# First pair of gate and up loads of each FFN block in eight half products, token sums made in stages

## The chip, the cores and the metric

The kernel runs on one core of one Trainium2 chip. The metric is the device time of one execution in microseconds; several timed runs are made, and their median counts. The engines are named as in the profile: PE (TensorE), DVE (VectorE), ACT (ScalarE), POOL (GpSimd), SP (SyncE, which issues the DMAs).

## The reference

The reference is one inference step of a decoder with two layers, on two groups of tokens: 512 prompt tokens and 64 tokens of samples with their states. A layer has four parts, each with a norm ahead and a residual add behind:

```python
x = x + 0.5 * swiglu(rmsnorm(x, ffn1_norm[l]), ffn1_w_gu[l], ffn1_w_down[l])
y, ... = even_mixer(...) or odd_mixer(...)      # on rmsnorm(x, mix_norm)
x = x + y
x = x + cross_attend(rmsnorm(x, xattn_norm[l]), mem_k[l], mem_v[l], xattn_wq[l], xattn_wo[l])
x = x + 0.5 * swiglu(rmsnorm(x, ffn2_norm[l]), ffn2_w_gu[l], ffn2_w_down[l])

def rmsnorm(x, g):
    return x * lax.rsqrt(jnp.mean(x * x, axis=-1, keepdims=True) + NORM_EPS) * g
def swiglu(x, w_gu, w_down):
    gate, up = jnp.split(x @ w_gu, 2, axis=-1)
    return (jax.nn.silu(gate) * up) @ w_down
```

The change touches the four calls of swiglu with the norm ahead of each. The model width is 1024 (8 chunks of 128), the hidden width 22 blocks of 128. All numbers are float32.

## The kernel before, in words

**Layout.** x stands transposed on the chip: xT has 8 chunks of 128 channels, each with 576 tokens, handled as two halves of TH = 288. A float32 product is made as three products of rounded parts: a number is split in a high part (ACT casts it to fp32r) and a low part (DVE subtracts the high part), and wh·xh + wh·xl + wl·xh is summed. One matmul is 128x128 by 128x288.

**FFN blocks.** There are four: A is ffn(0,1) at the start of the program, B is ffn(0,2) behind the output projection of layer 0's cross-attention, C is ffn(1,1) straight behind B's last down products, D is ffn(1,2) behind the cross-attention of layer 1. Each takes the 22 hidden blocks in parts (0,2), (2,6), ... (18,22). Two hidden blocks need a gate load and an up load, 1024x256 weights (1 MB) each, from two rotating buffers. `down` products (L1664) of a finished part are placed between the gate and up products of the next, and their results are added to xT by `add_x` (DVE, L1528).

**Seven products.** A load is multiplied with xT in a scheme of seven half-size products instead of eight (`seven`): the weights are seen as 2x2 blocks (odd and even chunks by the two column blocks), the tokens as blocks B11, B12, B21, B22 (odd and even chunk by token half). Seven weight forms (three blocks and four sums, the sums on DVE at L1609 and L1611) meet seven token forms: B11, T1, B21, T4, T2, B22 and T3, where the T are sums of blocks. Each product is `product` (L348): 12 matmuls, 4 chunk pairs by three parts; `seven` is 84 matmuls. DVE then puts the seven results together (L519 to L535, L1627, L1629). Each weight form is cast by ACT (L1578) and its low part made by DVE (L1579); forms rotate through two tags with three buffers each, so up to six are made ahead.

**Norm.** The tokens are not normalised ahead of the product: the products take x times the norm's gain, and the result is multiplied by rstd, the inverse root mean square. `norm_chunk` is called for a chunk as soon as xT's chunk is final: it makes the token forms (`token_forms`, all seven, 11 operations of DVE and 8 of ACT for a pair of chunks), and the square of x on ACT (L435), which POOL adds up into acc (L437; in A some on DVE). `norm_finish` multiplies acc by ones on PE (L479, which is behind the first two products of the FFN), takes Ln and Exp on ACT (L481, L482, each with a load of its function table), and corrects on DVE (L483, L485, L486). The gate result is multiplied by rstd (L519, L522), silu is taken on ACT (L526), and POOL multiplies by rstd once more (L528), for the up result that comes next (L532 to L535).

**Order.** `Stream` writes down a list of entries (one product or down product each) with posts (what DVE, ACT and POOL do with the results) and hooks; `emit` goes through it and `pin` ties the order on every engine. Behind each entry `make` makes forms ahead as far as buffers allow, and issues loads.

Of the kernel before, what the change touches and what calls it, by code (L numbers as in the profile page):

```python
# [140 lines left out]
class Net:  # L141
# [209 lines left out]
    def token_forms(self, c, name, base, late):  # L351
        nc = self.nc
        if c == 0:
            self.xf, self.late = {}, []
            for f in self.TOKENS_EARLY + self.TOKENS_LATE:
                h, l = (self.kp.tile([P, 2 * T], F32R, tag="y", bufs=6, name=self.nm("y")) if f in self.TOKENS_LATE else
                        self.kp.tile([P, 2 * T], F32R, tag=f"x{i}", bufs=4, name=self.nm("x")) for i in range(2))
                self.xf[f] = tuple(t.rearrange("p (j t) -> p j t", j=4) for t in (h, l))
        if c % 2 == 0:
            return  # L360
        j = c // 2
        (x11, x12), (x21, x22) = ((self.xT[:, k, :TH], self.xT[:, k, TH:]) for k in (c - 1, c))
        g1, g2 = self.vec(name, base + c - 1), self.vec(name, base + c)
        ta, tb = self.v2(self.ct('g1')), self.v2(self.ct('t0'))
        t1, t2, t4, t3 = ta[:, 0], ta[:, 1], tb[:, 0], tb[:, 1]

        def put(f, src, g):
            h, l = (t[:, j] for t in self.xf[f])
            if g is None:
                nc.scalar.copy(h, src)  # L370
                nc.vector.tensor_sub(l, src, h.bitcast(F32))
            else:
                nc.scalar.activation(h, src, AF.Identity, scale=g)
                nc.vector.scalar_tensor_tensor(l, src, g, h.bitcast(F32), ALU.mult, ALU.subtract)

        nc.vector.tensor_sub(t1, x12, x11)
        put('B11', x11, g1)
        nc.scalar.activation(t1, t1, AF.Identity, scale=g1)
        put('T1', t1, None)
        put('B21', x21, g2)  # L380
        nc.vector.scalar_tensor_tensor(t2, x22, g2, t1, ALU.mult, ALU.subtract)
        nc.vector.scalar_tensor_tensor(t4, x21, g2, t2, ALU.mult, ALU.subtract)
        put('T4', t4, None)

        def rest():
# [1400 lines left out]
```

## Time and profile before

| | us |
|---|---|
| timed runs | 3028.22, 3013.51, 3014.17 |
| their median | 3014.17 |
| the profiled execution's own time | 2999.72 |
| its span | 2997.9 |
| PE busy in it | 2866.5 (96%) |
| DVE busy | 2193.1 (73%) |
| ACT busy | 1280.0 (43%) |
| POOL busy | 419.8 (14%) |

The profile is of one execution, and its own time lies below the timed runs' median. The share of busy time is a mean over stages with different limits: the starts of the FFN blocks are at about 14, 995, 1400 and 2580 us of the span. The first gate load, first up load, second gate load and second up load of a block are called its first, second, third and fourth load. A start-to-end time of a run of instructions in the timeline (x24) includes what lies between them.

### The profile page before, as it was taken

To read this page: it belongs to the slowest core of one execution; us is meant where nothing else is said; L and a number is where in the kernel's file an instruction comes from. 1 tells how busy PE (TensorE), PEld (TensorE's weight loads), DVE (VectorE), ACT (ScalarE), POOL (GpSimd) and SP (SyncE) were. 2 spreads that over 40 slices of the span, in tenths; PEclk is the share of its full clock that TensorE was granted. 3 is DMA by queue.
4 is the path that set the end of the run, shared out by engine and by line. 5 is a ranking of instruction groups with operands and counts; after the bars stand their busy time and mean duration, and the time that the engine had idled before them with its cause. 6 is when DMAs were issued, how large, how long until landed. Compare 5 with 4: busy or idle time off the path is not lost.

```text
span 2997.9 us, 54618 instructions
## 1 busy us (share of the span) xinstructions
PE 2866.5 (96%) x22180; PEld 2707.4 (90%) x22180; DVE 2193.1 (73%) x3927; ACT 1280.0 (43%) x2302; POOL 419.8 (14%) x387
## 2 busy tenths in 40 slices
PE   5999999999999999997999999999999999999998
PEld 5999999999988899997999999988767787899998
DVE  7988866656556998887988875566577546898884
ACT  5544443222535544445444444433253534544443
POOL 1111011111100110001100011123222110110001
PEclk7999999999999999999999999999889999999999
DMA  3322232222445222221232232222113235232221
GB/s 113 111 93 85 89 85 72 72 82 93 145 167 175 75 95 92 87 87 61 89 99 89 89 96 78 81 60 81 38 34 92 86 142 192 73 97 89 92 81 64
DMA packets 343251, 278.76 MB, mean 93 GB/s; under 512 B 27332, under 2 KB 326168, under 8 KB 343000
## 3 DMA queue, kind: packets, MB, share of 16 engines
q1 hardware_dynamic: 343000, 275.27, 29.1%
q8 instruction: 175, 2.87, 0.4%
q14 instruction: 76, 0.62, 0.1%
HBM read 262.09 MB, written 13.14 MB: 92 GB/s over the span
## 4 chain that ended last, share of the span: by engine, by line
PE 81%; DVE 10%; ACT 4%; issue 2%; POOL 2%; DMA 1%; SPq 0%; ACTq 0%; POOLq 0%; DVEq 0%
PE pm L348 24%; PE pd L331 20%; PE pd L1664 17%; PE pd L348 4%; DVE wf L1579 2%; PE pm L968 1%; PE pm L891 1%; PE pd L1390 1%; PE pd L1359 1%; PE pd L1358 1%; PE pd L1360 1%; PE pm L1483 1%; PE pm L1452 1%; POOL acc L437 1%; PE pm L479 1%
## 5 line engine op out<-in xcount | busy, mean ns | idle before, releaser
L348 PE MATMUL pm<-x,wf 128*128 128x288 f32 x4224 | 606.8, 299 | 36.2 <-DVE wf L1579 14.5
L348 PEld LDWEIGHTS pm<-x,wf 128*128 128x128 f32 x4224 | 583.6, 191 | 41.9 <-DVE wf L1579 15.1
L331 PE MATMUL pd<-x,wh 128*128 128x288 f32 x2368 | 432.6, 302 | 0.0
L331 PEld LDWEIGHTS pd<-x,wh 128*128 128x128 f32 x2368 | 356.2, 191 | 5.4 <-ACT wh L317 0.9
L1664 PE MATMUL pd<-m,wf 128*128 128x288 f32 x2112 | 338.9, 296 | 12.1 <-DVE t L1629 8.2
L1528 DVE SCALAR_TENSOR_TENSOR xT<-pd,xT 128x576 f32<-128x576 f32 x240 | 181.2, 756 | 216.5 <-PE pd L1664 186.1
L1664 PE MATMUL pd<-g,wf 128*128 128x288 f32 x2112 | 337.5, 295 | 0.0
L528 POOL TENSOR_TENSOR g<-g,rstd 128x576 f32<-128x576 f32 x88 | 148.6, 1708 | 1271.9 <-DVE wf L1579 565.3
L1664 PEld LDWEIGHTS pd<-m,wf 128*128 128x128 f32 x2112 | 300.8, 188 | 14.2 <-ACT m L403 9.0
L348 PE MATMUL pm<-y,wf 128*128 128x288 f32 x2112 | 305.6, 295 | 0.3 <-ACT t L1625 0.3
L1664 PEld LDWEIGHTS pd<-g,wf 128*128 128x128 f32 x2112 | 299.2, 188 | 0.2
L348 PEld LDWEIGHTS pm<-y,wf 128*128 128x128 f32 x2112 | 289.5, 188 | 0.9 <-ACT t L1625 0.8
L1578 ACT CAST wf<-raw 128x512 fp32r<-128x512 f32 x264 | 163.1, 620 | 290.3 <-PE pd L1664 161.2
L331 PE MATMUL pd<-x,wl 128*128 128x288 f32 x1184 | 261.7, 302 | 0.0
L1578 ACT CAST wf<-t 128x512 fp32r<-128x512 f32 x264 | 163.8, 622 | 207.4 <-PE pm L348 82.4
L317 ACT CAST wh<-raw 128x1024 fp32r<-128x1024 f32 x106 | 111.1, 1048 | 274.2 <-PE pd L331 248.4
L1579 DVE TENSOR_TENSOR wf<-raw,wf 128x512 fp32r<-128x512 f32 x264 | 204.7, 776 | 11.3 <-ACT wf L1578 11.3
L1579 DVE TENSOR_TENSOR wf<-t,wf 128x512 fp32r<-128x512 f32 x264 | 193.2, 732 | 7.4 <-ACT wf L1578 7.4
L331 PEld LDWEIGHTS pd<-x,wl 128*128 128x128 f32 x1184 | 193.6, 191 | 1.8
L1578 ACT CAST wf<-S 128x512 fp32r<-128x512 f32 (+1 forms) x192 | 112.6, 587 | 161.4 <-PE pm L348 77.2
L331 PE MATMUL pd<-y,wh 128*128 128x288 f32 x896 | 169.6, 305 | 0.3 <-DVE xT L1528 0.3
L348 PE MATMUL pd<-y,wf 128*128 128x288 f32 x1056 | 155.8, 295 | 2.8 <-DVE wf L1579 2.8
(529 smaller groups left out, 4863.0 us busy)
## 6 DMA issues: line engine op xcount, KB each, us to landing
raw<-ffn_w_gu SPq DMA_DIRECT2D x88, 1024.0 KB
S<-ffn_w_down SPq DMA_DIRECT2D x160, 256.0 KB
raw<-xattn_wkv SPq DMA_DIRECT2D x16, 1024.0 KB
x<-cache_mem_v SPq DMA_DIRECT2D x32, 512.0 KB
raw<-cache_mem_k SPq DMA_DIRECT2D x16, 1024.0 KB
raw<-odd_w_in SPq DMA_DIRECT2D x30, 512.0 KB
raw<-even_w_in SPq DMA_DIRECT2D x16, 512.0 KB
raw<-xattn_wq SPq DMA_DIRECT2D x8, 1024.0 KB
```

The costliest lines, as they stand in the source:

```text
L317: nc.scalar.copy(h, raw[:, :, c:c + step])
L331: nc.tensor.matmul(ps[:, hf, :TH], w[:, k], x[:, hf * TH:(hf + 1) * TH], start=(k == 0 and w is wh and xi == 0), stop=(k == nk - 1 and w i ...
L348: self.nc.tensor.matmul(ps, a[:, j], b[:, j], start=(not more and j + i == 0), stop=(j == n - 1 and i == 2), skip_group_check=more)
L437: eng.tensor_add(self.acc, self.acc, sq)
L479: nc.tensor.matmul(ps[hf][:, :TH], lhsT, sq[:, hs])
L528: nc.gpsimd.tensor_mul(t, t, self.rstd)
L891: self.nc.tensor.matmul(ps[:, :TH], lhsT, rhs[:, hf * TH:(hf + 1) * TH])
L968: self.nc.tensor.matmul(ps[q, c * 64:(c + 1) * 64], *fn(c, q))
L1528: self.nc.vector.scalar_tensor_tensor(x, ps, s, x, ALU.mult, ALU.add)
L1578: self.nc.scalar.copy(h, src)
L1579: self.nc.vector.tensor_sub(l, src, h.bitcast(F32))
L1664: nc.tensor.matmul(ps[:, hf, :TH], a[:, k], b[:, hf * TH:(hf + 1) * TH], start=(k + i == 0), stop=(k == nk - 1 and i == 2))
```

## The change

In each FFN block the first pair of loads is multiplied in the plain way (`plain`, new): for each of the two column blocks, two half products (odd and even chunks), each with both token halves, so eight half products of 12 matmuls for a load (four entries of 24). It needs the four plain token blocks and four weight forms, no sums of weights. The gate's two halves gather in a double bank (psd) and are scaled by one operation of 576 elements, the up's in two single banks.

`norm_chunk` makes only the plain blocks (`token_blocks`: 4 operations of DVE and 4 of ACT for two chunks). The token sums T1, T2, T4 and T3 are made in eight stages (`token_sums`) as posts of the first pair's entries, the last two in the second gate load. silu is taken for each column block apart, and the first hidden blocks are split in the third load. The norm's matmuls go to two psm banks, and stand behind the second entry (A: the third). In A all sums of squares are on DVE. Hooks run ahead of posts.

```diff
-    TOKENS_EARLY, TOKENS_LATE = ('B11', 'T1', 'B21', 'T4'), ('T2', 'B22', 'T3')
-    def token_forms(self, c, name, base, late):
...
+    def token_blocks(self, c, name, base):
         if c == 0:
+            self.xf = {f: self.token_tiles(f, True) for f in ('B11', 'B12', 'B21', 'B22')}
+            self.xg = name, base
+        g, x = self.vec(name, base + c), self.xT[:, c]
+        for f, src in ((f'B{1 + c % 2}1', x[:, :TH]), (f'B{1 + c % 2}2', x[:, TH:])):
+            self.form_hi(self.xf, f, c // 2, src, g)
+            self.form_lo(self.xf, f, c // 2, src, g)
+    def token_sums(self, xf):
...
+        def first():
+            xf.update({f: self.token_tiles(f, False) for f in ('T1', 'T2', 'T4')})
+            d['t'] = [self.v2(self.ct('g1')) for _ in four]
+            for j in four:
+                nc.vector.tensor_sub(d['t'][j][:, 0], x[2 * j][1], x[2 * j][0])
+                nc.scalar.activation(d['t'][j][:, 0], d['t'][j][:, 0], AF.Identity, scale=g[2 * j])
+
+        def second():
+            for j in four:
+                t = d['t'][j]
+                self.form_hi(xf, 'T1', j, t[:, 0])
+                nc.vector.scalar_tensor_tensor(t[:, 1], x[2 * j + 1][1], g[2 * j + 1], t[:, 0], ALU.mult, ALU.subtract)
...
+        def seventh():
+            xf['T3'] = self.token_tiles('T3', True)
+            for j in four:
+                t = d['t'][j][:, 1]
+                nc.vector.scalar_tensor_tensor(t, x[2 * j][0], g[2 * j], t, ALU.mult, ALU.subtract)
+                self.form_hi(xf, 'T3', j, t)
...
-            ps = [self.psm(), self.psm()]
+        ps = [self.psm(1 if paired else None), self.psm(1 if paired else None)]
...
+                if t is None:
+                    nc.vector.tensor_mul(self.v2(z[n]), a, self.v2(self.rstd))
...
             if m0 == 0:
-                hooks = {1: finish, 6: loads} if then else {1: finish}
+                ts = [lambda n=n: steps[n]() for n in range(8)]
+                st.plain(wg, x, gate, [[ts[0]], [ts[1]], [], [ts[2], lambda: gated(0)]], {2: finish, 3: loads} if then else {1: finish}, False)
+                st.plain(wu, x, up, [[], [lambda: gated(1), ts[3]], [ts[4]], [ts[5]]], {}, True)
+                st.waiting += [(9, ts[6]), (10, done), (11, ts[7])]
+                return
...
-            self.square(c, self.nc.gpsimd if c % 3 == 1 else self.nc.vector)
+            self.square(c, self.nc.vector)
...
+    def plain(self, src, x, put, posts, hooks, single):
...
+                    for j in range(4):
+                        for i in range(3):
+                            for t in range(2):
+                                xs = x[row + str(t + 1)]
+                                self.nc.tensor.matmul(d['ps'][t][:, :TH], (wh, wh, wl)[i][:, j], xs[i == 1][:, j],
+                                                      start=(k + j + i == 0), stop=(k == 1 and j == 3 and i == 2))
...
             self.pin(e['run'], e['form']['w'])
-            post(e['posts'])
             if e['hook']:
                 e['hook']()
+            post(e['posts'])
             self.make(k)
```

Lines move by the change: L1528 becomes L1566, L1578 and L1579 become L1616 and L1617, L1611 becomes L1649, L479 becomes L509, L483 to L486 become L513 to L516, L532 (the up result times the gate's) becomes L566. New are L367 (low part of a plain block), L365 (low part of a sum), L389 and L396 (first two token sums), L549 (the gate's scaling of a whole block), and L1710 (the matmul of `plain`).

**Where the instructions move.** First, DVE at the end of B, where the last down products of B are added to xT and C's norm is fed. Between two residual adds (xT<-pd) stood, before, the token forms of a pair of chunks (x and y are their tiles, g and t scratch):

```order
L1528 SCALAR_TENSOR_TENSOR xT<-pd_14989,xT 128x576
L374 SCALAR_TENSOR_TENSOR x_14917<-xT,vecn,x_14916 128x288
L381 SCALAR_TENSOR_TENSOR g_15044<-xT,vecn,g_15044 128x288
L374 SCALAR_TENSOR_TENSOR x_14921<-xT,vecn,x_14920 128x288
L371 TENSOR_TENSOR x_14919<-g_15044,x_14918 128x288
L382 SCALAR_TENSOR_TENSOR t_15045<-xT,vecn,g_15044 128x288
L371 TENSOR_TENSOR y_14925<-g_15044,y_14924 128x288
L374 SCALAR_TENSOR_TENSOR y_14927<-xT,vecn,y_14926 128x288
L388 SCALAR_TENSOR_TENSOR t_15045<-xT,vecn,g_15044 128x288
L371 TENSOR_TENSOR x_14923<-t_15045,x_14922 128x288
L1528 SCALAR_TENSOR_TENSOR xT<-pd_15018,xT 128x576
```

Now, in the same place (xf are tiles of token blocks, wf weight forms, raw the gate load of C's first pair):

```order
L1566 SCALAR_TENSOR_TENSOR xT<-pd_14908,xT 128x576
L1617 TENSOR_TENSOR wf_15088<-raw_15081,wf_15088 128x512
L367 SCALAR_TENSOR_TENSOR xf_14859<-xT,vecn,xf_14858 128x288
L367 SCALAR_TENSOR_TENSOR xf_14861<-xT,vecn,xf_14860 128x288
L1566 SCALAR_TENSOR_TENSOR xT<-pd_14941,xT 128x576
L1617 TENSOR_TENSOR wf_15091<-raw_15081,wf_15091 128x512
L367 SCALAR_TENSOR_TENSOR xf_14855<-xT,vecn,xf_14854 128x288
L367 SCALAR_TENSOR_TENSOR xf_14857<-xT,vecn,xf_14856 128x288
L1566 SCALAR_TENSOR_TENSOR xT<-pd_14974,xT 128x576
```

Nine operations on 288 tokens stood between two adds; now there are three, and one of them is a weight form of the next block.

Second, DVE in B around the first operation on rstd. Before (acc's result is pd_10617):

```order
L371 TENSOR_TENSOR y_10061<-g_10507,y_10060 128x288
L374 SCALAR_TENSOR_TENSOR y_10063<-xT,veca,y_10062 128x288
L388 SCALAR_TENSOR_TENSOR t_10508<-xT,veca,g_10507 128x288
L371 TENSOR_TENSOR x_10059<-t_10508,x_10058 128x288
L1611 TENSOR_TENSOR t_10581<-g_10576,raw_10554 128x512
L371 TENSOR_TENSOR y_10065<-t_10508,y_10064 128x288
L1579 TENSOR_TENSOR wf_10583<-t_10560,wf_10583 128x512
L483 SCALAR_TENSOR_TENSOR t_10616<-rstd_10615 128x576
L485 SCALAR_TENSOR_TENSOR t_10616<-pd_10617,t_10616 128x288 x2
L486 SCALAR_TENSOR_TENSOR rstd_10615<-t_10616,rstd_10615 128x576
L1611 TENSOR_TENSOR t_10627<-raw_10554,t_10581 128x512
```

Now:

```order
L389 TENSOR_TENSOR g_10523<-xT 128x288
L513 SCALAR_TENSOR_TENSOR t_10557<-rstd_10556 128x576
L515 SCALAR_TENSOR_TENSOR t_10557<-pm_10558,t_10557 128x288
L515 SCALAR_TENSOR_TENSOR t_10557<-pm_10559,t_10557 128x288
L516 SCALAR_TENSOR_TENSOR rstd_10556<-t_10557,rstd_10556 128x576
L396 SCALAR_TENSOR_TENSOR g_10520<-xT,veca,g_10520 128x288
L396 SCALAR_TENSOR_TENSOR g_10521<-xT,veca,g_10521 128x288
L396 SCALAR_TENSOR_TENSOR g_10522<-xT,veca,g_10522 128x288
L396 SCALAR_TENSOR_TENSOR g_10523<-xT,veca,g_10523 128x288
L1649 TENSOR_TENSOR t_10579<-g_10484,raw_10479 128x512
L1617 TENSOR_TENSOR wf_10581<-raw_10465,wf_10581 128x512
L549 TENSOR_TENSOR g_10609<-pd_10489,rstd_10556 128x576
```

The token forms stood ahead of rstd; now a subtraction of token halves stands there, and the scaled sums (L396) and the gate's scaling (L549) follow behind it.

Third, PE in B around the norm's matmuls on acc. Before, they stood behind two products of 12 with token tiles x and banks pm:

```order
L348 MATMUL pm_10599<-x_10054,wf_10567 128x288 x2
L348 MATMUL pm_10599<-x_10055,wf_10567 128x288
L348 MATMUL pm_10599<-x_10054,wf_10567 128x288
L479 MATMUL pd_10617<-acc_10051,cblob 128x288 x2
L348 MATMUL pm_10586<-x_10056,wf_10570 128x288
L348 MATMUL pm_10586<-x_10057,wf_10570 128x288
```

Now, behind two entries of 24 in the double bank pd_10489 and ahead of the second column block's, pd_10584:

```order
L1710 MATMUL pd_10489<-xf_10028,wf_10470 128x288
L1710 MATMUL pd_10489<-xf_10025,wf_10470 128x288
L1710 MATMUL pd_10489<-xf_10027,wf_10470 128x288
L509 MATMUL pm_10558<-acc_10020,cblob 128x288
L509 MATMUL pm_10559<-acc_10020,cblob 128x288
L1710 MATMUL pd_10584<-xf_10021,wf_10473 128x288
L1710 MATMUL pd_10584<-xf_10023,wf_10473 128x288
L1710 MATMUL pd_10584<-xf_10022,wf_10473 128x288
```

There are 24 matmuls ahead of the norm's in B before, and 48 now.

## Rows read from the trace of the kernel before

**Rows 1.** The page's part 1: busy us (share) xinstructions, by engine.
```profile
PE 2866.5 (96%) x22180; PEld 2707.4 (90%) x22180; DVE 2193.1 (73%) x3927; ACT 1280.0 (43%) x2302; POOL 419.8 (14%) x387
```

**Rows 2.** Windows: stretch, its us, busy (xinstructions) by engine, PEclk, DMA, GB/s.
```profile
14.00:70.00 56.00, 31.32 (x175) 27.88 (x172) 47.08 (x90) 35.82 (x68) 8.71 (x5) 0.70 0.25 78
...
995.50:1029.07 33.57, 26.15 (x174) 24.37 (x173) 29.87 (x48) 21.12 (x38) 8.54 (x5) 0.95 0.13 43
...
1029.00:1098.00 69.00, 68.93 (x507) 68.96 (x508) 67.77 (x123) 32.18 (x62) 7.76 (x4) 0.98 0.31 100
```

**Rows 3.** Waits of PE: waiting <- released by: us, times, longest us.
```profile
PE pd L479 <- POOL acc L437: 16.6, 3, 8.9
...
PE pm L348 <- DVE wf L1579: 14.5, 2, 11.9
...
PE pd L1664 <- DVE xT L1528: 2.2, 2, 1.2
```

**Rows 4.** Timeline of PE in A: start, us, line, operation, [idle before <-releaser].
```profile
17.79 0.85 PE L348 MATMUL pm<-x,wf 128*128 128x288 f32 x2 [3.65 <-ACT wf L1578]
...
45.26 2.29 PE L479 MATMUL pd<-acc,cblob 128*128 128x288 f32 x4 [8.94 <-POOL acc L437]
...
70.19 5.08 PE L348 MATMUL pm<-x,wf 128*128 128x288 f32 x25 [1.87 <-DVE g L532]
```

**Rows 5.** Timeline of PE in B, a later down product last.
```profile
995.53 3.35 PE L348 MATMUL pm<-x,wf 128*128 128x288 f32 x24
...
1002.73 2.29 PE L479 MATMUL pd<-acc,cblob 128*128 128x288 f32 x4 [3.85 <-POOL acc L437]
...
1029.07 8.15 PE L348 MATMUL pm<-x,wf 128*128 128x288 f32 x48 [1.86 <-DVE g L532]
...
1099.29 0.96 PE L1664 MATMUL pd<-m,wf 128*128 128x288 f32 x6
```

**Rows 6.** Timeline of PE at the start of C.
```profile
1400.36 0.43 PE L348 MATMUL pm<-x,wf 128*128 128x288 f32 x2
...
1412.66 4.48 PE L348 MATMUL pm<-x,wf 128*128 128x288 f32 x22 [11.87 <-DVE wf L1579]
...
1416.97 1.13 PE L479 MATMUL pd<-acc,cblob 128*128 128x288 f32 x4
...
1442.35 6.62 PE L348 MATMUL pm<-x,wf 128*128 128x288 f32 x48 [1.40 <-DVE g L532]
```

**Rows 7.** Chain of waits in B: start, us, what.
```profile
1043.61 3.20 PE pm L348 x24
```

**Rows 8.** Timeline of ACT in B's norm.
```profile
1005.10 1.28 ACT L481 ACT_TABLE_LOAD   x1 [0.42 <-PE pd L479]
...
1008.60 0.69 ACT L482 ACTIVATE rstd<-t 128x576 f32<-128x576 f32 x1
```

**Rows 9.** Timeline of DVE in A, B and C.
```profile
50.50 0.76 DVE L483 SCALAR_TENSOR_TENSOR t<-rstd 128x576 f32<-128x576 f32 x1 [6.84 <-ACT rstd L482]
...
992.97 1.19 DVE L371 TENSOR_TENSOR y<-g,y 128x288 fp32r<-128x288 f32 x3
...
994.20 1.38 DVE L374 SCALAR_TENSOR_TENSOR y<-xT,veca,y 128x288 fp32r<-128x288 f32 x3
...
1009.39 0.76 DVE L483 SCALAR_TENSOR_TENSOR t<-rstd 128x576 f32<-128x576 f32 x1 [3.24 <-ACT rstd L482]
...
1022.99 1.92 DVE L1579 TENSOR_TENSOR wf<-t,wf 128x512 fp32r<-128x512 f32 x1
...
1042.05 0.76 DVE L1528 SCALAR_TENSOR_TENSOR xT<-pd,xT 128x576 f32<-128x576 f32 x1 [0.24 <-PE pd L1664]
...
1098.35 0.68 DVE L1579 TENSOR_TENSOR wf<-S,wf 128x512 fp32r<-128x512 f32 x1
...
1413.12 1.28 DVE L1579 TENSOR_TENSOR wf<-raw,wf 128x512 fp32r<-128x512 f32 x2
...
1422.48 0.76 DVE L483 SCALAR_TENSOR_TENSOR g<-rstd 128x576 f32<-128x576 f32 x1 [5.54 <-ACT rstd L482]
```

More of the change, by code (lines that the diff above doesn't have):

```diff
@@ L349, in product @@
                                       stop=(j == n - 1 and i == 2), skip_group_check=more)
-    def token_forms(self, c, name, base, late):
-        nc = self.nc
-        if c == 0:
[L354 to L385, printed above, removed]
-            put('T2', t2, None)
-            put('B22', x22, g2)
-            nc.vector.scalar_tensor_tensor(t3, x11, g1, t2, ALU.mult, ALU.subtract)
-            put('T3', t3, None)
-        self.late.append(rest)
-        if c == KD - 1 or not late:
-            for r in self.late:
-                r()
-            self.late = []
@@ new lines, in token_tiles, with form_hi @@
+    def token_tiles(self, f, plain):
+        h, l = (self.kp.tile([P, 2 * T], F32R, tag=f"x{i}" if plain else "y", bufs=4 if plain else 6,
+                             name=self.nm("xf")) for i in range(2))
+        return tuple(t.rearrange("p (j t) -> p j t", j=4) for t in (h, l))
+    def form_hi(self, xf, f, j, src, g=None):
+        h = xf[f][0][:, j]
+        if g is None:
+            self.nc.scalar.copy(h, src)
+        else:
+            self.nc.scalar.activation(h, src, AF.Identity, scale=g)
@@ L405, in split, with norm_chunk @@
         return h, l
-    def norm_chunk(self, c, name, base, squares=True, late=False):
+    def norm_chunk(self, c, name, base, squares=True):
         nc = self.nc
@@ L498, in ffn @@
         st = Stream(self)
-        x, rest = {}, []
+        x, rest, steps = {}, [], []
         def loads():
@@ L568, in ffn @@
         x.update(self.xf)
+        steps.extend(self.token_sums(x))
         st.emit()
@@ L1646, in seven, with make, run @@
                 self.place(job)
+    def plain(self, src, x, put, posts, hooks, single):
+        net = self.net
+        u = dict(src=src, steps=4, first=len(self.forms))
+        self.units.append(u)
+        for n in range(2):
+            d = {}
+            for k in range(2):
+                def make(tag, n=n, k=k):
+                    v = u['raw'].rearrange("p (j two) f -> p two j f", two=2)
+                    return self.form(v[:, k, :, n * P:(n + 1) * P], tag)
+                def run(w, n=n, k=k, d=d):
+                    if not k:
+                        if single:
+                            d['ps'] = [net.psm(n), net.psm(n)]
+                        else:
+                            d['pd'] = net.psd()
+                            d['ps'] = [d['pd'][:, 0], d['pd'][:, 1]]
+                    (wh, wl), row = w, f'B{k + 1}'
+                    for j in range(4):
[4 more added lines that the diff above has]
+                                                      start=(k + j + i == 0), stop=(k == 1 and j == 3 and i == 2))
+                e = self.entry(dict(make=make), run, hooks.get(2 * n + k))
+                self.entries[e]['posts'] += posts[2 * n + k]
+            if single:
+                for t in range(2):
+                    self.pending.append(lambda n=n, d=d, t=t: put(n, t, d['ps'][t][:, :TH], None, None))
+            else:
+                self.pending.append(lambda n=n, d=d: put(n, None, d['pd'][:, :, :TH], None, None))
     def full(self, src, xin, nk, m, add):
```

63 lines of the change are left out of this document (45 added, 18 removed).

## The prediction

> **What bounds the kernel now.** I read the page's busy line first, then the waits of TensorE (PE), then the four FFN starts in PE's timeline, then windows over them, and last VectorE's (DVE's) timeline. The four FFN blocks are called A (program start), B, C and D here.
>
> PE is busy 96% of a span of 2997.9 us [rows 1], so the kernel as a whole can only gain where PE stops. The list of its waits [rows 3] has two of the longest at FFN starts: PE waits 16.6 us in 3 waits for the sum of squares (acc, L437), and 14.5 us in 2 for weight forms (L1579). In time order they stand at A (8.94 us before L479), B (3.85), C (11.87 before the second part of its first product) [rows 4 to 6]; what is left of the 16.6, 3.8 us, is D, which is laid out like B.
>
> Why PE stops there is seen in the windows [rows 2]: between the end of the product ahead of B and B's third load, 33.57 us, PE works 26.15 us and DVE 29.87; in the 69 us that follow DVE works 67.77. So an FFN start is a stretch in which DVE makes token forms, weight sums and the low halves of weights, and PE is held by that list; after it DVE has no slack for some 70 us. At B its weight form of 1098.35 ends at 1099.03, and the down product that reads it starts at 1099.29: a lead of 0.26 us [rows 9, 5]. What counts is therefore not PE's own earliest time but how much earlier DVE reaches the point from which both kernels have the same DVE order, the weight forms of the fourth load.
>
> **What the change costs on PE.** Seven half products of 12 matmuls become eight in two loads of four FFNs: 2 × 12 × 4 = 96 matmuls more. 24 of them take 3.20 us back to back [rows 7], 0.133 us each: +12.8 us of PE work. It falls wholly into the stretches with the stops, 3.2 us in each.
>
> **What it does to DVE and ScalarE ahead of rstd.** Before, a pair of chunks costs 11 DVE operations ahead of the norm, now 4; the first pair's 8 weight sums in each FFN go, and of 14 forms 8 stay. The sums over tokens come after, in steps. The norm's two matmuls (L479, now L509) stand behind 48 half-product matmuls in B, C and D, behind 72 in A.
>
> B: the first product starts at 995.53 [rows 5] as before, since it needs only plain blocks. 48 × 0.133 = 6.4, so L509 comes at 1001.9; acc, held before by the longer list on DVE and ScalarE, is there by then. L509 takes 1.13 us at full clock (its row in C) [rows 6]. Then ScalarE: from the table load at 1005.10 to the end of Exp at 1009.29 are 4.2 us, of which the first 1.28 us table load waited for PE and now has time ahead of it; 2.9 stay [rows 8]. With 0.6 for the handovers, DVE's first operation on rstd starts at 1006.5 where it was 1009.39 [rows 9]: 2.9 us earlier. D the same.
>
> C: the nine DVE operations between two residual adds become three, so the two stops of PE for xT (2.2 us [rows 3]) go, nearly: 1.7. The first product then starts at 1398.7 in place of 1400.36 and does not stop for 11.87 us, as its four forms are made from the raw load in the tail. L509 at 1405.1, plus 1.1, 2.9 and nothing else late: rstd at 1409.1 where it was 1422.48 [rows 9]: 13.4 us earlier.
>
> A: the plain blocks of all chunks stand ahead of the first form, so I put the first product at 20.0 (17.79 before [rows 4]). 72 matmuls are 9.6 us at full clock. In the window 14 to 70 the mean granted clock was 0.70 [rows 2], and after the stop at 45.26 the four L479 matmuls took 2.29 us, against 1.13 in C: PE there ran at the lower level, 1.2 GHz, after idling. I add 2.8 us for such a beginning, 1 for late token blocks: L509 at 33.4, rstd on DVE at 33.4 + 1.1 + 2.9 = 37.4, I take 37.6 against 50.50 [rows 9]: 12.9 us earlier. If all 72 run at the lower level it is 6.8 us less.
>
> **What it costs behind rstd.** From rstd to the fourth load's second form DVE had 53 operations, now 60: nine 128x512 fewer, two 128x288 tensor operations, twelve 128x288 scalar-tensor-tensor and two 576-wide ones more. By rows with several in a run [rows 9] these are 0.64, 0.40, 0.46 and 0.76 us (the single 576-wide row): -5.8 + 0.8 + 5.5 + 1.5 = +2.1 us. Both ends: +0.8, if GpSimd's multiplications meet one operation fewer (the form at 1022.99 beside one took 1.92 us, 1.28 more than 0.64), and +4.7 if they meet two more. I take +1.5, nearer the lower end, because a run of two or three shows the overlap of neighbours only in part, and the removed kind is the longest. In A four of the scalar-tensor-tensor and two 128x512 stand ahead of rstd: 4 × 0.46 + 2 × 0.64 = 3.1 less behind it.
>
> On what these meetings cost, the Trainium skill ("SBUF — State Buffer", section "Who interferes with whom") says that a VectorE instruction with two SBUF inputs contends with a GpSimd one that reads SBUF, the port pair being an exclusive lock. The row of 1022.99 agrees in kind. The new scalar-tensor-tensor operations have two SBUF inputs too, so by that rule the change exposes more of DVE's list: if each of the eight first-pair multiplications cost one further 1.28 us, the sum would be 20 in place of 30 us and the median 2994.
>
> Moved work that I cost at nothing: the split of the first hidden blocks now stands in the third load, ahead of downs that start later; loads are issued no later, since a plain load frees its buffer after four forms; in A the constants' DMAs move three entries ahead, and SP waits there anyway for buffers. If that cover is gone PE waits at the third load, as it does today for L532 (1.86 us at 1029.07 [rows 5]); I keep that wait in all four.
>
> **The sum**, at the fourth load: A 12.9 + 3.1 - 1.5 = 14.5; C 13.4 - 1.5 = 11.9; B and D 2.9 - 1.5 = 1.4 each, plus the 0.24 us that DVE idled at 1042.05 and the lead of 0.26 [rows 9], 1.9 each. Together 30.2 us. That the gain is kept: PE and DVE move together from there, in the same order. PE alone does not limit it: B's 192 matmuls and L509 end at 995.53 + 25.5 + 1.1 = 1022.2, with the 1.9 wait 1024.1, 5.0 earlier than 1029.07; C at 1398.7 + 26.6 + 1.9 = 1427.2, 15.1 earlier than 1442.35; A at 20.0 + 2.8 + 1 + 26.6 + 1.9 = 52.3, 17.9 earlier than 70.19 [rows 4 to 6].
>
> The profiled execution took 2999.72 us, its span 2997.9; by its rows the new one takes about 2969.5. The timed runs have a median of 3014.17 (3013.51 to 3028.22), 14 above it, so the median forecast is 3014.17 - 30.2 = 2984.
>
> **Rivals.**
> 1. DVE gives more back: +4.7 behind rstd in place of +1.5. A 11.3, C 8.7, B and D below zero by 1.3 each: 17.4 us, 2997. For it: DVE's 67.77 of 69 us. Against: at B the list has only two GpSimd multiplications to meet, as before. Between this and the forecast lies 2990.
> 2. PE sets the end, because forms are made up to six ahead and DVE catches up where ScalarE or PE released it late: 17.9 + 5.0 + 15.1 + 5.0 = 43 us, 2971. For it: 0.24 us of idle time shows that PE paces DVE a little. Against: a lead of 0.26 us.
> 3. The slower side: the granted clock falls at FFN starts. Eight products with waits between them (two psm banks for the up product, each released by L566) leave PE short stops; where it then runs at 1.2 GHz, a matmul costs 0.133 us more. 227 matmuls at that level eat the 30.2 us; all 192 of each of B, C and D would cost 76.8, 3061. For it: the 24 matmuls and L479 after stops in A and B ran at the lower level, and 48 matmuls after the 1.86 us stop took 8.15 us where C took 6.62 after 1.40 [rows 5, 6]. Against: the stops removed are the long ones (8.94, 11.87, 3.85).
> 4. The stops do not go, only move behind the third load, since rstd is not what DVE waits for: then the 12.8 us are paid and nothing is won, 3027, within what counts as no change.
>
> **How the numbers follow.** Forecast 0.50, rival 1 0.20, rival 2 0.13, rival 3 0.06, rival 4 0.11. A measurement of this kernel can tell about 0.5%, 15 us, from no change: faster means below 2999, slower above 3029. The forecast and rival 2 are faster, and most of rival 1: 0.50 + 0.13 + 0.18 = 0.81. Same: rival 4 and the rest of 1, 0.13. Slower: rival 3, 0.06. The forecast's own range is 2976 to 2992 (A's clock, the two ends behind rstd); with rivals 1 and 2 it reaches 2968 to 3004, which leaves out rivals 3 and 4.
>
> **What would show it.** Right: no wait for acc or weight forms over 1 us at the starts of B, C and D; DVE's rstd operation near 37.6, 1006, some 13 us earlier in C's own frame, with a list of about 32.5 us behind it; PE work up by 12.8 us and its idle time down by about 43. Wrong: a wait for L566 or L365 above 3 us in the first pair, a clock below 0.9 in B's first 30 us, or a new wait for weight forms in the 70 us behind the third load, which would mean that the gain is given back there.

## The result, and the profile after

| | before | after |
|---|---|---|
| median of the timed runs, us | 3014.8 (3013.51 to 3028.22) | 2978.12 (2972.74 to 2981.82) |
| ratio after/before, 95% interval | | 0.9867 (0.9833 to 0.9901) |
| the profiled execution, its span | 2999.72, 2997.9 | 2981.82, 2980.0 |

The change is faster by 1.3%. The forecast was 2984 us, 30 us less than before; the medians differ by 36.7 us, the two profiled executions by 17.9. In the profiled pair the block starts gain 29.4 us and the two mixers give part of it back, as is shown below; of the other timed runs there is no trace.

The page's part 1 of the new profile (busy us, share of the span, instructions by engine), which answers to [rows 1]:

```profile
PE 2882.4 (97%) x22276; PEld 2725.2 (91%) x22276; DVE 2128.0 (71%) x3842; ACT 1266.0 (42%) x2278; POOL 419.9 (14%) x384
```

PE works 15.9 us more. 12.8 were worked out from 96 matmuls, but 10.4 of the 15.9 lie in the mixer of layer 1 (783.92 against 773.55 us in the rows of e0 below), which has the same 6697 matmuls in both and ran at a lower granted clock. The span is 17.9 us shorter, and PE's idle time fell from 131.4 to 97.6 us. DVE works 65 us less.

The windows of A's start and, from B's first product, 33.57 us, answering to the first two of [rows 2] (columns: stretch, its us, busy of PE, PEld, DVE, ACT, POOL, PEclk, DMA share, GB/s):

```profile
14.00:70.00 56.00, 45.93 (x301) 44.67 (x300) 49.61 (x95) 37.81 (x74) 4.50 (x3) 0.88 0.31 98
985.22:1018.79 33.57, 31.96 (x238) 31.53 (x237) 27.22 (x51) 20.81 (x39) 7.66 (x3) 1.00 0.16 52
```

In B's stretch PE works 31.96 us where it worked 26.15, and its granted clock is 1.00 where it was 0.95; in A's the clock is 0.88 where it was 0.70.

PE's waits (us in total, times, longest us), answering to [rows 3]:

```profile
PE pm L347 <- DVE g L566: 11.1, 5, 4.5
...
PE pm L347 <- ACT t L1663: 4.6, 3, 1.5
...
PE pd L347 <- DVE xf L365: 3.6, 4, 0.9
...
PE pm L347 <- ACT wf L1616: 3.2, 4, 0.8
...
PE pm L509 <- DVE acc L471: 1.1, 1, 1.1
```

The waits for acc at the FFN starts (16.6 us) and for weight forms (14.5) are gone, and that for xT in C's tail; 1.1 us for acc is left, in A. The program's first product still waits 3.3 us for ScalarE's cast. The wait for the up result has grown (L566, 11.1 us in 5, four of them at the starts, where L532 had 7.5 us in 5), and, not foreseen, there are three kinds of short ones in the third and fourth loads.

PE at the starts of A, B (its last row is the down product that answers to the last of [rows 5]) and C:

```profile
17.42 12.34 PE L1710 MATMUL pd<-xf,wf 128*128 128x288 f32 x72 [3.25 <-ACT wf L1616]
30.81 1.24 PE L509 MATMUL pm<-acc,cblob 128*128 128x288 f32 x4 [1.06 <-DVE acc L471]
...
52.51 11.91 PE L347 MATMUL pm<-xf,wf 128*128 128x288 f32 x72 [4.53 <-DVE g L566]
```

```profile
985.22 6.53 PE L1710 MATMUL pd<-xf,wf 128*128 128x288 f32 x48
991.60 1.14 PE L509 MATMUL pm<-acc,cblob 128*128 128x288 f32 x4
...
1013.45 8.25 PE L347 MATMUL pm<-xf,wf 128*128 128x288 f32 x60 [1.61 <-DVE g L566]
...
1086.46 0.96 PE L1737 MATMUL pd<-m,wf 128*128 128x288 f32 x6
```

```profile
1385.62 6.53 PE L1710 MATMUL pd<-xf,wf 128*128 128x288 f32 x48
1391.99 1.14 PE L509 MATMUL pm<-acc,cblob 128*128 128x288 f32 x4
...
1413.93 8.26 PE L347 MATMUL pm<-xf,wf 128*128 128x288 f32 x60 [1.70 <-DVE g L566]
```

In C the first product now runs without a stop into the norm, where it waited 11.87 us [rows 6]; in B the norm's matmuls wait for nothing, where they waited 3.85 [rows 5]. What is left in these rows are the stops ahead of the third load: 4.53 us in A, 1.61 in B, 1.70 in C.

DVE in A, B and C: the first operation on rstd in each, and rows of B ahead of it and behind it, answering to [rows 9]:

```profile
37.78 0.76 DVE L513 SCALAR_TENSOR_TENSOR t<-rstd 128x576 f32<-128x576 f32 x1 [3.51 <-ACT rstd L512]
```

```profile
988.16 1.93 DVE L1617 TENSOR_TENSOR wf<-raw,wf 128x512 fp32r<-128x512 f32 x1
...
996.61 0.76 DVE L513 SCALAR_TENSOR_TENSOR t<-rstd 128x576 f32<-128x576 f32 x1 [5.05 <-ACT rstd L512]
...
1008.26 2.96 DVE L407 SCALAR_TENSOR_TENSOR g<-xT,veca,g 128x288 f32<-128x288 f32 x4
1012.24 0.69 DVE L1617 TENSOR_TENSOR wf<-raw,wf 128x512 fp32r<-128x512 f32 x1 [1.02 <-ACT wf L1616]
...
1028.71 0.68 DVE L1617 TENSOR_TENSOR wf<-g,wf 128x512 fp32r<-128x512 f32 x1
...
1030.62 0.74 DVE L1566 SCALAR_TENSOR_TENSOR xT<-pd,xT 128x576 f32<-128x576 f32 x1
```

```profile
1397.10 0.76 DVE L513 SCALAR_TENSOR_TENSOR g<-rstd 128x576 f32<-128x576 f32 x1 [5.05 <-ACT rstd L512]
```

From B's first product to DVE's operation on rstd are now 996.61 - 985.22 = 11.39 us, before 1009.39 - 995.53 = 13.86. In C it is 11.48, before 22.12; in A 20.36, before 32.71.

**Where the time came from.** The same event stands in both traces, so the lead of the new kernel can be followed from place to place:

| event (PE or DVE) | before, us | after, us | lead, us |
|---|---|---|---|
| A's first residual add | 83.67 | 70.53 | 13.1 |
| B's first FFN product | 995.53 | 985.22 | 10.3 |
| a down product of B | 1099.29 | 1086.46 | 12.8 |
| C's first FFN product | 1400.36 | 1385.62 | 14.7 |
| ninth residual add of C | 1512.84 | 1488.76 | 24.1 |
| D's first FFN product | 2579.56 | 2563.50 | 16.1 |
| ninth residual add of D | 2685.14 | 2666.53 | 18.6 |

The four starts gain 13.1 (A), 2.5 (B), 24.08 - 12.83 = 11.2 (C, with B's tail), and 2.6 (D, 18.61 - 16.06): 29.4 us. Between them, in the mixers and cross-attention, 2.8 us of the lead went in layer 0 and 8.0 in layer 1. The change edits no line of the mixers.

### The profile page after: what moved, and what is told of

Its sections match the earlier page's. It is cut to its first block, busy times and chain, and to the rows that moved or that the text cites. A ratio compares the mean times of both kernels' runs of the same rounds, so it can differ in the third digit from the quotient of the medians.

```text
span 2980.0 us, 54645 instructions
## 1 busy us (share of the span) xinstructions
PE 2882.4 (97%) x22276; PEld 2725.2 (91%) x22276; DVE 2128.0 (71%) x3842; ACT 1266.0 (42%) x2278; POOL 419.9 (14%) x384
## 4 chain that ended last, share of the span: by engine, by line
PE 82%; DVE 9%; ACT 4%; issue 2%; POOL 1%; DMA 1%; SPq 0%; ACTq 0%; POOLq 0%; DVEq 0%
PE pm L347 23%; PE pd L331 21%; PE pd L1737 18%; PE pd L347 4%; DVE wf L1617 2%; PE pm L1006 2%; PE pm L929 1%; PE pd L1428 1%; PE pd L1397 1%; PE pd L1396 1%; PE pd L1398 1%; PE pm L1521 1%; PE pm L1490 1%; PE pm L1506 1%; DVE xf L365 1%
## 5 line engine op out<-in xcount | busy, mean ns | idle before, releaser
L347 PE MATMUL pm<-xf,wf 128*128 128x288 f32 x5760 | 807.3, 296 | 19.0 <-DVE g L566 11.1
L347 PEld LDWEIGHTS pm<-xf,wf 128*128 128x128 f32 x5760 | 781.5, 188 | 22.5 <-ACT wf L1616 16.1
L1566 DVE SCALAR_TENSOR_TENSOR xT<-pd,xT 128x576 f32<-128x576 f32 x240 | 181.2, 755 | 253.7 <-PE pd L1737 189.8
L1616 ACT CAST wf<-raw 128x512 fp32r<-128x512 f32 x272 | 166.9, 619 | 300.3 <-PE pd L1737 168.1
L1616 ACT CAST wf<-t 128x512 fp32r<-128x512 f32 x240 | 149.0, 622 | 200.3 <-PE pm L347 76.2
L1617 DVE TENSOR_TENSOR wf<-raw,wf 128x512 fp32r<-128x512 f32 x272 | 208.9, 770 | 15.2 <-ACT wf L1616 15.0
L1617 DVE TENSOR_TENSOR wf<-t,wf 128x512 fp32r<-128x512 f32 x240 | 174.3, 726 | 10.3 <-ACT wf L1616 10.3
L1616 ACT CAST wf<-S 128x512 fp32r<-128x512 f32 (+1 forms) x192 | 112.6, 587 | 157.9 <-PE pm L347 69.2
L347 PE MATMUL pd<-xf,wf 128*128 128x288 f32 x960 | 141.9, 295 | 3.6 <-DVE xf L365 3.6
L331 PEld LDWEIGHTS pd<-y,wh 128*128 128x128 f32 x896 | 136.7, 193 | 4.0 <-DVE xT L1566 0.5
L318 DVE TENSOR_TENSOR wl<-raw,wh 128x1024 fp32r<-128x1024 f32 x106 | 130.6, 1232 | 10.9 <-ACT wh L317 6.9
```

The lines of the kernel that those rows point to most:

```text
L318: nc.vector.tensor_sub(l, raw[:, :, c:c + step], h.bitcast(F32))
L331: nc.tensor.matmul(ps[:, hf, :TH], w[:, k], x[:, hf * TH:(hf + 1) * TH], start=(k == 0 and w is wh and xi == 0), stop=(k == nk - 1 and w i ...
L347: self.nc.tensor.matmul(ps, a[:, j], b[:, j], start=(not more and j + i == 0), stop=(j == n - 1 and i == 2), skip_group_check=more)
L1566: self.nc.vector.scalar_tensor_tensor(x, ps, s, x, ALU.mult, ALU.add)
L1616: self.nc.scalar.copy(h, src)
L1617: self.nc.vector.tensor_sub(l, src, h.bitcast(F32))
```

## The experiments

All runs are measured in the same way: a block's frame is the time from its first product (PE, L1710) to its first residual add (DVE, L1566), in B 1030.62 - 985.22 = 45.40 us; beside it stands the time to DVE's first operation on rstd (L513). Frames of the changed kernel repeat to a tenth of a microsecond between two profiles, while its timed executions differ by up to 19 us.

| kernel | frame A | B | C | D | rstd A | B | C | D |
|---|---|---|---|---|---|---|---|---|
| after | 53.11 | 45.39 | 45.48 | 45.39 | 20.36 | 11.39 | 11.48 | 11.39 |
| e0, the same again | 53.16 | 45.40 | 45.48 | 45.39 | 20.36 | 11.39 | 11.48 | 11.40 |
| e1, later norm | 53.15 | 45.29 | 45.30 | 45.26 | 20.37 | 13.34 | 13.34 | 13.34 |
| e2, 24 matmuls fewer | 53.13 | 44.34 | 45.45 | 45.38 | 20.37 | 10.32 | 11.48 | 11.40 |
| e3, earlier norm | 51.05 | 42.22 | 42.33 | 42.24 | 17.21 | 8.21 | 8.30 | 8.21 |
| e4, list shortened | 53.15 | 43.69 | 44.44 | 43.68 | 20.37 | 11.40 | 11.48 | 11.40 |
| e5, squares on GpSimd | 54.95 | 45.40 | 45.49 | 45.39 | 22.17 | 11.40 | 11.48 | 11.39 |
| e7, e3 and T4's stage later | 51.06 | 41.18 | 41.28 | 41.19 | 18.26 | 8.22 | 8.31 | 8.22 |
| e8, e7 and the square first | 50.65 | 40.34 | 40.33 | 40.35 | 17.85 | 7.37 | 7.37 | 7.38 |

**e0, b0, b1: what one and the same kernel does.** No edit: the changed kernel once more, the kernel before twice more.

> The changed kernel once more, unedited. Frame used for all runs: from a block's first half product to the start of the first residual add inside the block (A 53.1, B 45.4, C 45.5, D 45.4 us in the first profile). Theory 1 (the block starts are set by DVE's list behind rstd, and the 11 us given back between B's end and D's start in the first profile are the clock of that one execution): the four frames repeat within 0.3 us, while the stretches of the two mixers differ by several us between profiles of one and the same kernel. Theory 2 (the change itself delays the mixers, by the norm's new banks or the DMA order): the mixers come out as late against the kernel before as in the first profile, 2.8 us in the first and 8 us in the second.

> The kernel before once more, unedited. Frames are taken from a block's first FFN product to the first residual add inside the block, and were 65.9, 46.5, 54.6 and 46.5 us in A, B, C, D in the first profile; the sum of what the change gains at the four starts and in C's tail was 29.4 us, while the medians of the timed runs differ by 37 us. Theory 1: the frames repeat within 0.5 us, and the rest of the difference lies in the two mixers (outside the FFN blocks), at a lower granted clock there: this profile is longer than the first by that alone. Rival: the frames of the kernel before vary by several us, and the first profile was a fortunate one.

> The kernel before a third time, for the same question: frames within 0.5 us of 65.9, 46.5, 54.6, 46.5 by theory 1; the mixers' stretches (0.4 to 0.95 ms and 1.77 to 2.56 ms) differ by several us between the three profiles of one and the same kernel.

The frames repeat, for the changed kernel within 0.1 us; for the kernel before they are 65.5, 45.8, 55.5 and 45.8 in b0 (3013.8 us) and 65.5, 46.2, 54.8 and 46.2 in b1 (3006.1 us), against 65.9, 46.5, 54.6 and 46.5: within 0.9, not the 0.5 expected. This bears on the sum of the gains: with the same changed profile, taken from A's first residual add and from the ninth adds of B, C and D, the four starts gain 12.7, 0.6, 12.9 and 0.6 us against b0 (26.8 in all) and 12.7, 1.0, 11.4 and 1.0 against b1 (26.2). In B and D the first profile, from which the forecast was worked out, was the slowest of the three.

The mixer of layer 1 does not repeat. From a residual add at C's end to D's first product, in five profiles (before, b0, b1, after, e0):

```profile
1771.44:2579.56 808.12, 773.55 (x6697) 669.44 (x6696) 503.37 (x1003) 332.83 (x600) 156.61 (x179) 0.95 0.29 88
```

```profile
1774.09:2595.74 821.65, 788.11 (x6697) 680.84 (x6696) 503.23 (x1003) 333.09 (x600) 155.92 (x179) 0.93 0.29 87
```

```profile
1772.30:2588.55 816.25, 779.71 (x6697) 674.47 (x6696) 502.87 (x1003) 332.95 (x600) 155.34 (x179) 0.94 0.29 88
```

```profile
1747.36:2563.50 816.14, 783.92 (x6697) 679.14 (x6696) 489.41 (x979) 329.02 (x591) 158.96 (x181) 0.94 0.29 88
```

```profile
1746.48:2546.47 799.99, 766.88 (x6698) 665.98 (x6696) 489.01 (x979) 329.18 (x591) 159.04 (x181) 0.96 0.30 90
```

The stretch took 808.1, 821.7 and 816.3 us in the kernel before and 816.1 and 800.0 in the changed one, and the shorter it was, the higher the granted clock (in the order of the rows 0.95, 0.93, 0.94, 0.94 and 0.96). Where the first profile of the changed kernel gave back 8.0 us in layer 1, e0 gained 808.12 - 799.99 = 8.1 there, without an edit between them: theory 1 holds, and the difference of the two first profiles is a bad measure of the change. That the timed medians differ by 36.7 and not by 29.4 is within what these stretches vary; whether the change makes them shorter on average, these profiles don't say. From C's ninth residual add to D's first product it is 1066.7 to 1080.3 us in the three profiles of the kernel before (mean 1073.9) and 1058.6 to 1077.3 in the nine that have the plain first pair (after and e0 to e8, mean 1070.8): the ranges overlap.

**e1: rstd later.** The hook of the gate load moves by one entry in B, C and D:

```diff
-                st.plain(wg, x, gate, ..., {2: finish, 3: loads} if then else {1: finish}, False)
+                st.plain(wg, x, gate, ..., {2: finish, 3: loads} if then else {2: finish}, False)
```

> In B, C and D the norm's matmuls stand behind 72 half-product matmuls instead of 48; no work is added or taken away; A is as it was. Theory 1 (DVE's list behind rstd sets the frame): rstd comes 24 x 0.133 = 3.2 us later, and the frames of B, C and D become 48.0 to 48.7 us, A stays at 53.1; in all about 9 us longer. Theory 2 (PE's own work sets the frame, the order of the norm does not matter): all frames stay within 0.3 us.

The frames did not grow, so the number expected by theory 1 missed, and theory 2's was met. The trace shows why this does not decide: rstd came only 1.95 us later, and with the hook three steps changed sides. DVE in B:

```profile
991.65 2.98 DVE L396 SCALAR_TENSOR_TENSOR g<-xT,veca,g 128x288 f32<-128x288 f32 x4
994.55 0.68 DVE L1649 TENSOR_TENSOR t<-g,raw 128x512 f32<-128x512 f32 x1
995.15 0.68 DVE L1617 TENSOR_TENSOR wf<-raw,wf 128x512 fp32r<-128x512 f32 x1
999.98 0.76 DVE L513 SCALAR_TENSOR_TENSOR t<-rstd 128x576 f32<-128x576 f32 x1 [4.14 <-ACT rstd L512]
```

The four sums of L396, the weight sum (L1649) and the low half (L1617) now stand ahead of rstd, where DVE waited 5.05 us and now 4.14. The list behind it went from 34.0 us to 45.29 - 13.34 = 31.95. Arrival and list changed by the same 2 us.

**e2: less work for PE.** The kernel leaves out 24 of the 96 matmuls of each block's first up load. In the matmul loop of `plain`:

```diff
                         for i in range(3):
+                            if single and i == 1 and j:
+                                continue
```

> Leaves out part of the computation: in the first up load 24 of the 96 matmuls (the products with the low part of the tokens for three of four chunk pairs). PE then has as much work in the first pair as in the kernel before. Theory 1: the extra 12.8 us of PE work lie under DVE's list, so the frames shrink by less than 1 us each, and PE's stop for the up result (L566, 1.6 us in B) grows by about 3 us. Theory 2 (PE sets the frame): each frame is 3.2 us shorter, 42.2 in B, C and D.

In A, C and D the frames are the same to 0.03 us, and in B 1.05 us shorter with an rstd that came 1.07 us earlier. That lead is not the edit's: it is there ahead of the matmuls left out. In B the last square is added up on GpSimd while DVE makes a weight form. In the changed kernel DVE was held up there (1.93 us at 988.16, above), and GpSimd took 1.61 us; in e2 it was GpSimd, and DVE took 0.69 us, so that all of DVE's next steps came earlier. The row of the changed kernel, then two of e2:

```profile
987.92 1.61 POOL L471 TENSOR_TENSOR acc<-acc,t 128x576 f32<-128x576 f32 x1 [4.79 <-ACT t L469]
```

```profile
986.45 3.69 POOL L471 TENSOR_TENSOR acc<-acc,t 128x576 f32<-128x576 f32 x1 [4.79 <-ACT t L469]
986.69 0.69 DVE L1617 TENSOR_TENSOR wf<-raw,wf 128x512 fp32r<-128x512 f32 x1
```

PE waits longer instead:

```profile
PE pm L347 <- DVE g L566: 22.6, 5, 7.8
```

22.6 us where it was 11.1 in all: the 96 matmuls taken away came back as 11.5 us of waiting. So the extra work of the eight products lies under DVE's list, and theory 2 falls.

**e3: rstd earlier.** The hook moves to the first entry (B, C, D), the ACT half of the first stage goes behind it:

```diff
-                nc.scalar.activation(d['t'][j][:, 0], d['t'][j][:, 0], AF.Identity, scale=g[2 * j])
+
+        def scaled():
+            for j in four:
+                nc.scalar.activation(d['t'][j][:, 0], d['t'][j][:, 0], AF.Identity, scale=g[2 * j])
...
-                st.plain(wg, x, gate, [[ts[0]], [ts[1]], [], [ts[2], lambda: gated(0)]], {2: finish, 3: loads} if then else {1: finish}, False)
+                st.plain(wg, x, gate, [[ts[0]], [], [ts[8], ts[1]], [ts[2], lambda: gated(0)]] if then else
+                         [[], [ts[8], ts[1]], [], [ts[2], lambda: gated(0)]],
+                         {2: finish, 3: loads} if then else {0: lambda: (st.pin(ts[0]), finish())}, False)
```

> The norm earlier, no work added: in B, C and D its matmuls stand behind 24 half-product matmuls, and in all four blocks ScalarE's scaling of the first token sum is moved behind the norm, so that its table load and Ln no longer wait for it. Theory 1: rstd about 3 us earlier in B, C and D (L513's place from 11.4 to about 8.5 us after the block's start), 2 in A; frames 42.4 to 43.4 in B, C, D and about 51 in A; 8 to 11 us in all. Theory 2 (PE sets the frame): the frames stay. Theory 3 (acc is not ready so early: the wait for acc takes the place): L509 waits over 2 us for acc and the frames shrink by less than 1 us.

rstd came 3.18 us earlier in B, C and D, and the frames shrank by 3.15 to 3.17. DVE's order is the same there as in the changed kernel, so this is the test that e1 was meant to be. In A rstd came 3.15 us earlier and the frame shrank by 2.06: there the four scaled sums, ahead of rstd before, stand behind it now. PE in B:

```profile
980.94 3.35 PE L1715 MATMUL pd<-xf,wf 128*128 128x288 f32 x24
985.27 1.24 PE L512 MATMUL pm<-acc,cblob 128*128 128x288 f32 x4 [0.98 <-POOL acc L474]
986.13 9.93 PE L1715 MATMUL pd<-xf,wf 128*128 128x288 f32 x72
...
1008.64 9.76 PE L347 MATMUL pm<-xf,wf 128*128 128x288 f32 x72
```

The norm's matmuls wait 0.98 us for acc, and the third load starts without a stop. Timed, e3 is at 2963.44 us (ratio to before 0.986, 0.9823 to 0.9898).

**e4: the list shorter, rstd where it was.** L396's four operations become a step of their own, `t2`, emitted ahead of the norm's hook:

```diff
                 self.form_hi(xf, 'T1', j, t[:, 0])
+
+        def t2():
+            for j in four:
+                t = d['t'][j]
                 nc.vector.scalar_tensor_tensor(t[:, 1], x[2 * j + 1][1], g[2 * j + 1], t[:, 0], ALU.mult, ALU.subtract)
...
-                st.plain(wg, x, gate, [[ts[0]], [ts[1]], ...
+                st.plain(wg, x, gate, [[ts[0], ts[8]], [ts[1]], ...
```

> The changed kernel, with the four scaled sums of T2 (L396 there, 1.72 us of DVE from start to start) moved ahead of DVE's first operation on rstd in B, C and D, into the 5.05 us in which DVE waits for rstd; norm and PE untouched. In A they stand ahead of it already. The run with the later norm moved rstd and this part of the list at once, so it did not tell the theories apart; this one moves only the list. Theory 1 (frame = arrival of rstd + DVE's list behind it): rstd stays at 11.4 us, frames of B, C and D 43.7 us, A 53.1. Theory 2 (PE sets the frame): 45.4 as it was. Theory 3 (the frame hangs on rstd alone): 45.4 as well.

B 43.69 and D 43.68, as expected to 0.02 us, with rstd unmoved. C lost only 1.04: there a group of four low halves, 1.56 us in B, met a GpSimd multiplication that began at 1399.32.

```profile
1393.65 0.76 DVE L516 SCALAR_TENSOR_TENSOR g<-rstd 128x576 f32<-128x576 f32 x1 [3.34 <-ACT rstd L515]
...
1399.05 2.80 DVE L365 TENSOR_TENSOR xf<-g,xf 128x288 fp32r<-128x288 f32 x4
```

**e5: one bundled edit undone.**

```diff
-            self.square(c, self.nc.vector)
+            self.square(c, self.nc.gpsimd if c % 3 == 1 else self.nc.vector)
```

> The changed kernel with one bundled edit undone: in A three of the seven additions of squares go back to GpSimd. B, C and D are untouched (45.4). Theory 1: an addition takes about 1.4 us there and 0.75 on DVE, in one chain, so acc is 2 us later, rstd in A at about 22.4 in place of 20.4 us, and the frame of A at about 55 in place of 53.1: the edit is worth some 2 of A's 13 us. Rival: the additions leave DVE free for its list, and A comes out the same or shorter.

A's frame is 54.95 and rstd at 22.17; the other blocks stay. The first of the three additions on GpSimd (the others took 1.74 and 1.48 us):

```profile
24.09 1.43 POOL L471 TENSOR_TENSOR acc<-acc,t 128x576 f32<-128x576 f32 x1 [23.64 <-ACT t L469]
```

The edit is worth 1.8 of A's 13.1 us. It is the only bundled edit that a run undoes by itself: how the rest of the gain is shared between the eight products, the later token sums and the norm's new place is not shown.

**e7 and e8: what is left.** e7 is e3 with T4's stage behind the making of forms, e8 is e7 with the last chunk's square first:

```diff
-                st.plain(wu, x, up, [[], [lambda: gated(1), ts[3]], [ts[4]], [ts[5]]], {}, True)
+                st.plain(wu, x, up, [[], [lambda: gated(1)], [ts[4]], [ts[5]]], {}, True)
+                st.entries[-3]['late'] = [ts[3]]
...
             self.make(k)
+            post(e.get('late', []))
...
+        first = squares and name[:3] == 'ffn' and c == KD - 1
+        if first:
+            self.square(c, nc.gpsimd)
         if name[:3] == 'ffn':
...
-        if squares:
+        if squares and not first:
```

> The version with the early norm, and in addition the stage that makes T4's sums (L407 in the changed kernel) is emitted behind the next weight form instead of ahead of it, so that DVE does not wait 1.02 us for a cast of ScalarE queued behind it. Theory 1: frames of B, C and D 41.2 (42.2 with the early norm alone), A about 50; 4 us in all. Rival: the up result (L566) or T4's low part is then late, and the 1.0 us come back in another place: frames within 0.3 us of 42.2 and 51.05.

> The version with the early norm and the later stage of T4, and the square of the last chunk ahead of its token blocks on ScalarE, so that acc is there 0.96 us earlier in B, C and D, where PE waits 0.99 us for it. Theory 1, by now with PE as the next limit there (its 192 products and the norm are 26.6 us, and the third load follows without a stop): the stop for acc goes and the frames of B, C and D become 40.2 us; A stays at 51.06. Rival: the last chunk's token blocks are then late for the second entry and take the stop over: 41.2.

e7: 41.18, 41.28 and 41.19, and A 51.06 where about 50 was expected: there rstd came 1.05 us later than in e3, with a wait of 2.30 us for acc. e8: 40.3 in B, C and D. PE in B of e8:

```profile
984.86 3.35 PE L1719 MATMUL pd<-xf,wf 128*128 128x288 f32 x24
988.35 1.24 PE L515 MATMUL pm<-acc,cblob 128*128 128x288 f32 x4
989.21 9.94 PE L1719 MATMUL pd<-xf,wf 128*128 128x288 f32 x72
998.98 12.91 PE L1719 MATMUL pm<-xf,wf 128*128 128x288 f32 x96
1011.73 9.76 PE L347 MATMUL pm<-xf,wf 128*128 128x288 f32 x72
```

PE runs from the first product into the third load without a stop, and 5.1 us of frame have gone since the changed kernel. That PE sets the start now is not shown, though: from rstd to the end of the frame are 40.34 - 7.37 = 32.97 us in B, and 41.18 - 8.22 = 32.96 in e7, so the frame is still rstd's arrival and DVE's list. Timed, e7 is at 2966.28 (ratio to before 0.9852, 0.9818 to 0.9885) and e8 at 2957.64 us (0.9805, 0.9766 to 0.9844). e8's median is below those of both kernels; its runs (2946.98 to 2967.02) just overlap those of the changed kernel in e0 (2964.72 to 2983.32). Its sum of frames is 171.7 us against 189.4.

## Why the prediction was right

The time was forecast as 2984 (2968 to 3004) and is 2978.12. The sum was 30.2 us, and the trace has 29.4, or 26 to 27 if b0 or b1 stands for the kernel before:

| | forecast | measured, first profiles | against b0 | against b1 |
|---|---|---|---|---|
| A | 14.5 | 13.1 | 12.7 | 12.7 |
| B | 1.9 | 2.5 | 0.6 | 1.0 |
| C, with B's tail | 11.9 | 11.2 | 12.9 | 11.4 |
| D | 1.9 | 2.6 | 0.6 | 1.0 |

The mechanism is right. That the sum fits within 1 us is in part luck, as several terms below missed and made up for each other.

- **PE's extra work lies where it stood idle.** Right: e2 takes 24 matmuls away in each block and gains nothing in A, C and D, and in B no more than an earlier rstd gives.
- **DVE's list behind rstd sets the fourth load.** Right, by e3 (rstd earlier, list the same), e4 (list shorter, rstd the same) and e2. In B the frame less rstd's arrival is 34.0 us in the changed kernel, e0, e2, e3 and e5 alike, whether rstd came at 11.4, 10.3 or 8.2. e1 moved both and shows nothing by itself.
- **rstd.** In A 37.78 was measured (37.6 said), 20.36 us after the first product where it was 32.71. In B it came 2.5 us earlier than before (2.9 said), in C 12.5 (1422.48 less 1397.10 is 25.4, of which 12.8 is the lead at B's down product; 13.4 said, in a sum without the 0.6 us of handovers that B's has). The reason given for B was partly wrong: the first table load was to lie ahead of the norm's matmuls, with 2.9 us behind them. ScalarE in B:

```profile
990.49 1.81 ACT L390 ACTIVATE g<-g,veca 128x288 f32<-128x288 f32 x4 [2.71 <-DVE g L389]
992.32 1.28 ACT L511 ACT_TABLE_LOAD   x1
993.61 0.89 ACT L511 ACTIVATE t<-pm,eps 128x288 f32<-128x288 f32 x2
...
995.82 0.69 ACT L512 ACTIVATE rstd<-t 128x576 f32<-128x576 f32 x1
```

The table load stands behind the four scalings (L390) of the first token stage, which wait for DVE's subtractions, and begins at 992.32, 0.72 us after L509 began: Ln waits for it until 993.61. This is the place that e3 mends.
- **The list's growth** was taken as +1.5 us. From rstd to the fourth load's second form it was 30.42 us in B before (1009.39 to 1039.81 by the start of that form) and is 1028.71 - 996.61 = 32.10: +1.7. Between the bounds (0.8 and 4.7), and near the value taken, but by luck: two waits of DVE for ScalarE (1.02 us at 1012.24 and 0.71) were not in the working and are by themselves 1.7 us, so the operations, 53 before and 60 now, priced at +2.1, added about nothing.
- **The first product of A** was put at 20.0 and came at 17.42: the blocks were not late. Its 72 matmuls took 12.34 us (12.4 said, with 2.8 at the lower clock); what was gained there was lost to the wait for acc (1.06) and behind. L509 came at 30.81 where 33.4 was said, and from there to DVE's operation on rstd it was 6.97 us where 4.2 were said: that 37.78 lies by 37.6 is luck.
- **The stop kept ahead of the third load** was 1.9 us in the working; it is 1.61 in B, 1.70 in C and 4.53 in A. As PE is not the limit there, it costs nothing by itself (e2). A's is above the 3 us that the forecast named as a sign of being wrong within the first pair; it stands behind that pair. PE's idle time fell by 33.8 us where about 43 were said.
- **Rival 1** (DVE gives back 4.7): no. **Rival 2** (PE sets the end, 43 us): no; in e8 the third load follows without a stop in three blocks, but DVE's list still fits the frame. **Rival 3** (the clock falls at block starts): in B the reverse. B's start has a granted clock of 1.00, and the 60 matmuls behind its stop of 1.61 us took 8.25 us, full speed. In A the third load ran at 0.80 behind its stop of 4.53 us. **Rival 4**: no.

On the meetings of DVE and GpSimd, the rows of B are these, of GpSimd's two multiplications by rstd and of DVE beside and between them:

```profile
1003.41 4.38 POOL L560 TENSOR_TENSOR g<-g,rstd 128x576 f32<-128x576 f32 x1 [13.88 <-ACT g L558]
1007.95 1.67 POOL L560 TENSOR_TENSOR g<-g,rstd 128x576 f32<-128x576 f32 x1 [0.17 <-ACT g L558]
```

```profile
998.93 1.80 DVE L396 SCALAR_TENSOR_TENSOR g<-xT,veca,g 128x288 f32<-128x288 f32 x4
...
1007.07 1.26 DVE L1617 TENSOR_TENSOR wf<-g,wf 128x512 fp32r<-128x512 f32 x1
```

The second took 1.67 us, and the four L407 operations beside it 2.96 us, where four L396 operations took 1.80. The first took 4.38 us, and DVE's operations beside it their usual time but for the last, a weight form of 1.26 us where others take 0.68. The Trainium skill ("SBUF — State Buffer", section "Who interferes with whom") says that the shared port pair is an exclusive lock and that the order of issue decides who is held up. The rows agree that at a meeting one of the two is held up; by the times at which the two start they don't tell which, as at B's last square GpSimd began 0.24 us ahead of DVE's weight form both in the changed kernel, where DVE was held up, and in e2, where GpSimd was. The forecast put the eight multiplications at 10 us if each cost a further 1.28 us; in B the two held DVE up by 1.16 and 0.58 us, less than before, where they held it up by 1.24 (the 1.92 us at 1022.99 [rows 9]) and 1.13 us (a 128x512 operation of 1.81 us at 1024.95).

## What to carry to other kernels

An operation count on the engine that is busy 96% of the span may go up at no cost where that engine waits for another: read the stretch, not the share. Ask then what the waiting engine's list hangs on: here one scalar chain (sum of squares, matmul, two table loads, two activations), and in e3 and e8 each microsecond by which it came earlier shortened the starts of B, C and D by one; no run reached the point where PE takes over. Judge such a change by frames between events that both traces hold: they repeat to a tenth of a microsecond in the changed kernel and within 0.9 in the one before, while whole executions of one kernel differ by 20 us. And take more than one profile of the kernel before: worked out from another of its three, B and D would have gained 0.6 or 1.0 us in place of 2.5.
